# Value projection of the 1024-token set in three column groups (322, 484, 484) instead of four of 322, with the phase's on-chip memory laid out anew

## Chip, cores and metric

One core of a Trainium2 chip runs the whole layer in one launch. The metric is device time in microseconds, the median of three executions. Beside it there is one profiled execution with a trace of every instruction and every DMA.

## What is computed

The layer takes two token sets, x_prompt (1024 tokens) and x_sample (512 tokens), each of width 1024. All weights are shared. Cut to what matters here:

```python
h = rms_norm(x, pre_w)
cols = jnp.einsum('bsd,dc->bsc', h, w_in)          # one combined input projection
m_qk, m_v, m_o, m_z, m_i, m_f, a_qkv, a_z, gate = jnp.split(cols, np.cumsum(IN_SPLITS)[:-1], axis=-1)
y_m = mlstm_mixer(m_qk, m_v, m_o, m_i, m_f, ...) * silu(m_z)      # branch A, uses m_v and the 16 gate columns m_i, m_f
y_a = dilated_attention(a_qkv, rel_table) * silu(a_z)             # branch B, uses the 1536 value columns of a_qkv
merged = sig(g_A) * (y_m @ w_proj_m) + sig(g_B) * (y_a @ w_proj_a)
y = x + rms_norm(merged @ w_out, post_w)
```

The change concerns the first phase of the long set (1024 tokens): the projection of h on 2576 columns of w_in. These are 16 gate columns (m_i, m_f), 1024 columns of m_v and 1536 value columns of the attention.

## The kernel before

**Precision.** Every fp32 operand is split in a high part (a ScalarE copy to fp32r) and a low part (a VectorE subtraction, operand minus high part). `mm3` (L209 to L214) multiplies with three matmuls: high by high, high by low, low by high.

**Seven products.** The long set is two blocks of 512 tokens (rows) by two halves of the contraction (4 tiles of 128 each). The weights of a group are two halves of the contraction by two halves of columns. `value_group` (L452) forms the 2x2 block product with seven block products instead of eight (Winograd's form of Strassen's scheme). In the order of the later groups they are m1, m2, m6, m7, m5, m4, m3. Their left operands H[..][B11 .. B22] are sums of blocks of h, kept for the whole phase; their right operands are sums of weight blocks, made for each group. One product is 4 row tiles t by 4 contraction tiles k by 3 matmuls, so 48 matmuls. The moving operand is the weight block, VW = 322 columns wide, the stationary operand a 128x128 tile of H. A group of two column halves covers 2 x 322 columns; four groups, g = 0 to 3, cover 2576. Each row tile of a product accumulates in one PSUM bank; there are eight in a pool.

**What stands around a product.** `split` (L461) makes the high and low part of a weight block into one of two places (`vhi`, `vlo`, bufs=2), so a block can be split only after the product before the last one, in its place, has ended. `sums` (L442) and L609/L623 form the weight sums on VectorE. The evictions are VectorE additions of PSUM to SBUF tiles `u2`, `u3`, `co` (L626 to L671). `out` (L499) stores a finished piece of 128 rows by 322 columns: m_v columns as high and low parts (through tiles `vz`, `vzm`) to the DRAM tensor `vs`, attention columns to `av`. `opening` (L471) loads the raw weights of the next group with four DMAs on GpSimd's queue and splits its first block; it is called when m4 of a group is issued (L662). The `u2` tiles alternate between the names `u2` and `u2b` from group to group.

**Group 0** is special. Its products are interleaved with the making of H itself: transposes of x on TensorE (`put`, L415), evictions of these by ScalarE and VectorE (L430, L432), differences of the blocks of x (L409, L411). The x tiles of the first block (`x0`) lie in a pool of the left side, those of the second (`x1`) in one of the right side. The `u3` tiles of group 0 are the first 322 columns of the x0 tiles (L2270). The pool `co`, which reuses x1's memory, is opened after m6 (L614).

**Lanes and tables.** `lanes` (L946) makes the decay tables of the mLSTM from the gate columns. It is a generator of five stages with small TensorE transposes (L957, L990, L991, L1011, L1033, L1034) between chains on ScalarE and VectorE. L2284 to L2290 take its steps in groups 1 and 2, after every third product. `bias_tables` (L342) makes the relative-bias rows of the attention with two small matmuls (L356); it runs after the lanes, ahead of group 3.

**Order.** TensorE's instructions stand in the order in which the program issues them. The order on the other engines is planned when the program is built, from dependences and priorities; `issue_after` holds an instruction behind another one on its engine, and `split` has high priority. Memory of a closed pool is reused tile by tile: a new tile waits until the tiles that lay there are done with.

**After the values** come the pairs (L2296 on): `pair_weights` loads and splits two column units (`pw_raw`, `phla`, `phlb`, `psum_w`) in memory that the value weights held, and `unit_pair` multiplies with 512-wide moving operands. The last stores of group 3 go into the list `late` and are issued behind the first pair loads.

Of the kernel before, what the change touches and what calls it, by code (L numbers as in the profile page):

```python
# [29 lines left out]
P = 128  # L30
D = 1024
# [16 lines left out]
VW = 322  # L48
# [25 lines left out]
class Tokens:  # L74


    def __init__(self, dram, S, x, y, name):
        self.S, self.x, self.y, self.n, self.nblk, self.name = S, x, y, S // P, S // BLK, name
        t = lambda shape, what, dt=F32: dram.tile(shape, dt, name=f"{what}_{name}")
        self.qk = t([16, P, S], "qk")  # L80
        self.vs = t([2, S, D], "vs")
        self.G = t([8, P, S], "G")
        self.aqk = t([2, 24, P, S], "aqk")
        self.av = t([S, 1536], "av")
        self.az = t([4, P, S], "az")
# [3 lines left out]
        self.og = t([S, 3, 4, OW], "og")  # L89

# [93 lines left out]
class Net:  # L184
# [157 lines left out]
    def bias_tables(self, sb, ps, dram):  # L342
# [17 lines left out]
        nc.sync.dma_start(self.erow, e)  # L360

# [87 lines left out]
    def value_weights(self, sb):  # L449
        return [sb.tile([P, 2, 4 * VW], F32, name=x, bufs=1) for x in ("va", "vb", "vsum")]  # L450

    def value_group(self, g, T, H, sb, us, co, ps, late=None, begin=None, u3=None, more=None, turn=None):  # L452
# [6 lines left out]
        N = 4 * VW  # L459
        place = lambda: [sb.tile([P, N], F32R, name=x, bufs=2) for x in ("vhi", "vlo")]  # L460
        def split(x, at=None, parts=1):  # L461
            hi, lo = at or place()
            with self.tc.high_priority():
                for i in range(parts):
                    c = slice(i * N // parts, (i + 1) * N // parts)
                    ends = (nc.scalar.activation(hi[:, c], x[:, c], AF.Copy),
                            (nc.gpsimd if i else nc.vector).tensor_sub(lo[:, c], x[:, c], hi[:, c].bitcast(F32)))
            self.splits = ends
            return hi.rearrange("p (k c) -> p k c", c=VW), lo.rearrange("p (k c) -> p k c", c=VW)

        def opening(g):  # L471
            wa, wb = (sb.tile([P, 2, N], F32, name=x, bufs=1) for x in ("va", "vb"))
            for j, w in enumerate((wa, wb)):
                for kh in range(2):
                    nc.gpsimd.dma_start(w[:, kh], self.a["w_vp"][g, j, kh])
            return wa, wb, split(wa[:, 0]), self.splits[1]

        if g:
            wa, wb, w11, early = self.opened
            s = sb.tile([P, 2, N], F32, name="vsum", bufs=1)  # L480
        else:
            first, wa, wb, s, (lead, norm, sub, put) = begin

        def product(m, w, turns=(), outer=False, onto=None):

            banks = onto or [ps.tile([P, BLK], F32, name="d") for _ in range(4)]
            turns = iter(turns)
            if outer:
                next(turns)
            for i in range(4):  # L490
                for j in range(4):
                    t, k = (j, i) if outer else (i, j)
                    ts = slice(t * P, (t + 1) * P)
                    self.mm3(banks[t][:, :VW], (H[0][m][:, k, ts], H[1][m][:, k, ts]), (w[0][:, k], w[1][:, k]),
                             k == 0 and onto is None, k == 3, skip_group_check=onto is not None)
                next(turns, None)
            return banks

        def out(t, blk, jc, c):  # L499

            r = slice(blk * BLK + t * P, blk * BLK + (t + 1) * P)
            c0 = 2 * VW * g + VW * jc
            lo, hi = c0, c0 + VW
            if lo < 16:
                nc.scalar.activation(self.gates_of(T, blk * 4 + t), c[:, 0:16].rearrange("p (j h) -> p j h", h=4), AF.Copy)
            a0, a1 = max(lo, 16), min(hi, 16 + D)
            if a0 < a1:
                w = a1 - a0
                z = vz()
                x = c[:, a0 - c0:a1 - c0]  # L510
                nc.scalar.activation(z[:, 0, :w], x, AF.Copy)
                nc.vector.tensor_sub(z[:, 1, :w], x, z[:, 0, :w].bitcast(F32))
                store(T.vs[:, r, a0 - 16:a1 - 16].rearrange("a t c -> t a c"), z[:, :, :w].bitcast(F32))
            a0 = max(lo, 16 + D)
            if a0 < hi:
                store(T.av[r, a0 - 16 - D:hi - 16 - D], c[:, a0 - c0:])

        vz = lambda: (more.tile([P, 2, VW], F32R, name="vzm", bufs=2) if more and next(turn) < 2 else
                      co.tile([P, 2, VW], F32R, name="vz", bufs=3))
        tile_ = lambda name, bufs: (us if name[:2] == "u2" else co).tile([P, VW], F32, name=name, bufs=bufs)  # L520
        u2 = [tile_(("u2", "u2b")[g % 2], 4) for _ in range(4)]
        add = nc.vector.tensor_add
        if g == 0:
            lead()
            w11, low = split(wa[:, 0], first, 2), []
# [88 lines left out]
            co = co()  # L614
        else:
            with self.tc.issue_after(early.ins):
                self.sums(wa, wb, s)()
            m1 = product(B11, w11)
            for t in range(4):
                nc.scalar.activation(u2[t], m1[t][:, :VW], AF.Copy)  # L620
            w12 = split(wa[:, 1])
            s2 = split(s[:, 1])
            nc.vector.tensor_sub(s[:, 1], wa[:, 1], s[:, 1])  # L623
            yield
            m2 = product(B21, w12)
            co = co()  # L626
            for t in range(4):
                c = tile_("co", 3)
                add(c, u2[t], m2[t][:, :VW])
                out(t, 0, 0, c)  # L630
            yield
            m6 = product(T2, s2)
            for t in range(4):
                add(u2[t], u2[t], m6[t][:, :VW])
            yield
            m7 = product(T3, split(wb[:, 0]))
            u3 = []
            for t in range(4):
                u3.append(tile_("u3", 4))
                nc.vector.tensor_sub(u3[t], u2[t], m7[t][:, :VW])  # L640
            yield
        if g == 0:
            with self.tc.issue_after(low[2]):
                s1 = split(s[:, 0])
        else:
            s1 = split(s[:, 0])
        m5 = product(T1, s1)
        if g == 0:
            for t, c in enumerate(held):
                out(t, 0, 0, c)  # L650
        for t in range(4):
            add(u2[t], u2[t], m5[t][:, :VW])
            c = tile_("co", 3)
# [3 lines left out]
        if late is not None:  # L657
            store = lambda *x: late.append(x)
        m4 = product(T4, split(wb[:, 1]))
        if g < 3:  # L660
            w3 = split(s[:, 1])
            self.opened = opening(g + 1)  # L662
# [5 lines left out]
        m3 = product(B22, w3 if g < 3 else split(s[:, 1]))  # L668
# [277 lines left out]
    def lanes(self, T, sb, bank, apart=False):  # L946
# [8 lines left out]
        li, lf, e, u1, l, q1 = (t(x) for x in ("li", "lf", "e", "u1", "l", "u"))  # L955
# [1249 lines left out]
def body(tc, a):  # L2205
# [3 lines left out]
    with ExitStack() as st:  # L2209
# [12 lines left out]
        with ExitStack() as s1:  # L2222
# [4 lines left out]
            with ExitStack() as sv:  # L2227
                vw = N.pool(sv, "vw", 1, "left")
                us = N.pool(s2, "us", 1, "right")
                s3, s4 = ExitStack(), ExitStack()  # L2230
                begin = [vw.tile([P, 4 * VW], F32R, name=x, bufs=2) for x in ("vhi", "vlo")], *N.value_weights(vw)
# [3 lines left out]
                xp = N.pool(s3, "x0", 1, "left"), N.pool(s4, "x1", 1, "right")  # L2235
                xt = [[xp[i].tile([P, D], F32, name=f"x{i}{t}") for t in range(4)] for i in range(2)]
# [4 lines left out]
                weights = lambda j, kh: nc.sync.dma_start(begin[1 + j][:, kh], a["w_vp"][0, j, kh])  # L2241
# [28 lines left out]
                values = [N.value_group(0, A, H, vw, us, co, ps, None, (*begin, turns), [x[:, :VW] for x in xt[0]])]  # L2270
                next(values[0])
# [3 lines left out]
                for _ in values[0]:  # L2275
                    pass
                s3.close()
                more, turn = N.pool(sv, "more", 1, "left"), itertools.cycle(range(5))
                values += [N.value_group(g, A, H, vw, us, co, ps, late if g == 3 else None, more=more, turn=turn)
                           for g in range(1, 4)]  # L2280
# [221 lines left out]
```

## Time and profile before

| | |
|---|---|
| runs | 2199.57 us median of 3 (2198.99 to 2202.0) |
| profiled execution, its own time | 2196.68 us |
| its span, first to last instruction | 2194.8 us |
| granted TensorE clock, mean | 0.999 |
| PE busy, share of the span | 99% |
| DVE / ACT / POOL busy | 67% / 50% / 32% |
| DMA | 390.42 MB, mean 178 GB/s |

The profiled execution took 2.89 us less than the median of the runs, and 1.9 us more than its span. Busy TensorE is counted with the pipelined ends of matmuls, so the distance between the starts of two matmuls, not their busy time, is what a matmul costs. In the trace, the first phase of the long set runs from the start to the first matmul of the pairs at 235.25 us; of this, m5 of group 0 begins at 60.47 us.

### The profile page before, as it was taken

The page shows a single profiled execution, that of the slowest core. Times are in us where ns is not written, and L with a number is a line of the kernel's source. Part 1 is how long each engine was busy: PE and PEld are TensorE (multiplying, and loading weights), DVE is VectorE, ACT ScalarE, POOL GpSimd, SP SyncE. Part 2 cuts the span into 40 slices and gives each one's busy share as a digit, 9 for nine tenths or more (in the row PEclk, how much of TensorE's full clock was granted, in tenths as well). Part 3 has the DMA queues.
Part 4 walks back from the last instruction along what each step waited for, and adds up shares of the span by engine and source line. Part 5 has one row for each costly group of instructions (what it writes and reads, how often), then busy time and mean ns, then how long its engine had stood idle before and what let it go on. Part 6 is the DMA issues. An engine that isn't in the chain of part 4 may idle for free.

```text
span 2194.8 us, 34409 instructions
## 1 busy us (share of the span) xinstructions
PE 2180.1 (99%) x11962; PEld 1883.1 (86%) x11962; DVE 1460.9 (67%) x2970; ACT 1088.8 (50%) x2246; POOL 706.5 (32%) x994
## 2 busy tenths in 40 slices
PE   9999999999999999999999999999999999999998
PEld 8999888888888888888888889999788888888887
DVE  7775565657787555547888765574667855666673
ACT  7332243344444333446777656666755544554332
POOL 1000432333333222326776650011045522232331
PEclk9999999999999999999999999999999999999999
DMA  3842443433333222366646569997678786776772
GB/s 126 196 116 80 154 165 135 173 106 112 109 115 109 75 86 96 135 217 239 211 155 228 147 191 248 246 244 198 197 238 279 240 282 209 232 258 183 237 244 106
DMA packets 207640, 390.42 MB, mean 178 GB/s; under 512 B 37513, under 2 KB 121161, under 8 KB 207466
## 3 DMA queue, kind: packets, MB, share of 16 engines
q1 hardware_dynamic: 176584, 276.15, 40.5%
q0 software_dynamic: 27280, 99.48, 14.2%
q10 hardware_dynamic: 3602, 12.59, 1.4%
q8 instruction: 95, 1.56, 0.3%
q14 instruction: 79, 0.65, 0.1%
HBM read 274.70 MB, written 113.44 MB: 177 GB/s over the span
## 4 chain that ended last, share of the span: by engine, by line
PE 90%; DMA 4%; DVE 2%; issue 1%; ACT 1%; POOL 1%; SPq 0%; DVEq 0%; POOLq 0%; ACTq 0%
PE d L214 14%; PE d L212 14%; PE d L213 14%; PE dense L212 11%; PE dense L214 11%; PE dense L213 11%; PE lg L1695 1%; PE pt L1725 1%; PE num L212 1%; PE num L214 1%; PE num L213 1%; PE o L1768 1%; PE num L1390 1%; PE a L1097 1%; PE kv L212 1%
## 5 line engine op out<-in xcount | busy, mean ns | idle before, releaser
L212 PE MATMUL dense<-H,wh 128*128 128x512 f32 x664 | 269.4, 406 | 0.0
L213 PE MATMUL dense<-H,wh 128*128 128x512 f32 x664 | 260.4, 392 | 0.0
L214 PE MATMUL dense<-H,wl 128*128 128x512 f32 x664 | 260.3, 392 | 0.0
L213 PE MATMUL d<-Hl,phla 128*128 128x512 f32 x608 | 236.5, 389 | 0.0
L214 PE MATMUL d<-Hh,phla 128*128 128x512 f32 x608 | 236.5, 389 | 0.0
L212 PE MATMUL d<-Hh,phla 128*128 128x512 f32 x608 | 236.5, 389 | 0.0
L281 DVE TENSOR_TENSOR wl<-wraw,wh 128x1024 fp32r<-128x1024 f32 (+1 forms) x121 | 150.1, 1241 | 49.3 <-ACT wh L275 49.0
L214 PE MATMUL d<-Hh,phlb 128*128 128x512 f32 x456 | 177.4, 389 | 0.0
L212 PE MATMUL d<-Hh,phlb 128*128 128x512 f32 x456 | 177.4, 389 | 0.0
L213 PE MATMUL d<-Hl,phlb 128*128 128x512 f32 x456 | 177.4, 389 | 0.0
L275 ACT ACTIVATE wh<-wraw 128x1024 fp32r<-128x1024 f32 (+1 forms) x124 | 128.2, 1035 | 65.6 <-PE dense L213 21.9
L214 PEld LDWEIGHTS dense<-H,wl 128*128 128x128 f32 x664 | 124.7, 188 | 28.1
L697 POOL TENSOR_TENSOR psum_w<-pw_raw 128x512 f32<-128x512 f32 x38 | 55.3, 1455 | 283.3 <-DMA pw_raw<-w_in 266.0
L214 PE MATMUL d<-vhi,Hl 128*128 128x322 f32 x448 | 140.5, 314 | 0.5 <-DVE Hl L432 0.3
L212 PE MATMUL d<-vhi,Hh 128*128 128x322 f32 x448 | 140.3, 313 | 0.1
L213 PE MATMUL d<-vlo,Hh 128*128 128x322 f32 x448 | 139.6, 312 | 0.0
L212 PEld LDWEIGHTS dense<-H,wh 128*128 128x128 f32 x664 | 125.1, 188 | 16.5 <-issue 1.2
L213 PEld LDWEIGHTS dense<-H,wh 128*128 128x128 f32 x664 | 125.3, 189 | 14.7
L1714 DVE CUSTOM_DVE_ANT_0 ls<-lg,bias 128x256 f32<-128x256 f32 (+2 forms) x240 | 78.8, 352 | 85.5 <-PE lg L1695 63.7
L212 PEld LDWEIGHTS d<-Hh,phla 128*128 128x128 f32 x608 | 114.1, 188 | 23.7
L213 PEld LDWEIGHTS d<-Hl,phla 128*128 128x128 f32 x608 | 114.1, 188 | 23.7
L214 PEld LDWEIGHTS d<-Hh,phla 128*128 128x128 f32 x608 | 114.1, 188 | 23.6
(635 smaller groups left out, 5811.1 us busy)
## 6 DMA issues: line engine op xcount, KB each, us to landing
pw_raw<-w_in SPq DMA_DIRECT2D x76, 512.0 KB, 4.3
wraw<-w_in SPq DMA_DIRECT2D x63, 512.0 KB, 4.3
aqk_a<-pwk SPq DMA_DIRECT2D x40, 512.0 KB, 3.5
wraw<-w_pm POOLq DMA_DIRECT2D x24, 512.0 KB, 5.5
wraw<-w_out POOLq DMA_DIRECT2D x24, 512.0 KB, 4.0
aqk_b<-sw SPq DMA_DIRECT2D x40, 256.0 KB, 6.2
wraw<-w_v POOLq DMA_DIRECT2D x22, 430.0 KB, 7.2
qk_a<-pwk SPq DMA_DIRECT2D x16, 512.0 KB, 2.6
```

The source lines that it names most:

```text
L212: nc.tensor.matmul(out, lh, rh, start=start, stop=False, **kw)
L213: nc.tensor.matmul(out, lh, rl, start=False, stop=False, **kw)
L214: nc.tensor.matmul(out, ll, rh, start=False, stop=stop, **kw)
L275: high = nc.scalar.activation(hi[:, :n], raw[:, :n], AF.Copy)
L281: low = (self.lows or nc.vector).tensor_sub(lo[:, :n], raw[:, :n], hi[:, :n].bitcast(F32))
L697: self.nc.gpsimd.tensor_add(s[:, 0], ws[1][:, 0], ws[1][:, 1])
L1097: nc.tensor.matmul(p[:, c - c0], kT[:, ct, c * P:(c + 1) * P], qT[:, ct, c * P:(c + 1) * P], start=ct == 0, stop=ct == 1)
L1390: nc.tensor.matmul(pn, hi[:, j], z[:, c1], start=j == 0 and z is v[0], stop=False)
L1695: nc.tensor.matmul(lg[:, hh], q[hh][:, qs], z.rearrange("p (n j) -> p n j", j=P)[:, pair], start=z is k[hh], stop=z is not k[hh])
L1714: nc.vector.tensor_tensor_reduce(out=ls[rows, hh], in0=ts["lg"][hh][rows, of], in1=bt[rows, hh, by], scale=1.0, scalar=NEG, op0=OP.add, op ...
L1725: nc.tensor.transpose(pp[:, hh * nk + x], ts["ls"][:, hh, x * P:(x + 1) * P], self.ident)
L1768: nc.tensor.matmul(of(hh, 0, P), vh(kt[x], hh), pt[:, hh * len(kt) + x], start=x == 0, stop=x == len(kt) - 1)
```

## The change

The 2576 columns, padded to 2580, are cut in three groups: group 0 stays at 2 x 322 columns and its own code (`value_group`), and groups 1 and 2 take 2 x 484 columns each (`wide_group`). Each group still has seven products of 48 matmuls. `value_split` and `value_product` are the former inner functions `split` and `product`, made methods.

The memory is laid out anew. Four tiles v0 to v3 (8 x 484, 4 x 322, 16 x 484 and 4 x 1024 columns) take the place of `vhi`, `vlo`, `va`, `vb`, `vsum` and x0. In group 0 the places of the split weights lie in v0 and v1, the raw weights and sums in v2, the x0 tiles in v3. In the wide groups the two places of split weights lie in v3 and v0, the four raw blocks in v2, and the sum `ws`, the tiles `wu2` (4), `wco` (2), `wu3` (4) in a new pool on the right side, opened when group 0's pools close. The `wu2` tiles are the same four in both wide groups. The high parts of m_v pieces in group 1 go to three slices of v1 (`z_of`); the low parts are written in place of the piece. The u3 tiles of group 0 move from x0's columns to the pool `co`, which is now opened before the evictions of m7.

The lanes' steps all move into group 2, one after each product, with their tiles in v1 and a tile of the right pool; the bias tables move into group 2 too, their loads after m6, their matmuls after m5, with their tiles in the first raw block. The host lays out the weights for the new groups (`w_vp` for group 0, `w_vw` for the wide ones).

```diff
-VW = 322
+VW, WW = 322, 484
...
+    def wide_open(self, g, wide):
+        if g == 1:
+            quarter = lambda x, i: x[:, i * 4 * WW:(i + 1) * 4 * WW]
+            places = [[quarter(x, i).bitcast(F32R) for i in range(2)] for x in (wide(3), wide(0, False))]
+            self.wide = itertools.cycle(places), [quarter(wide(2, False), i) for i in range(4)]
+        places, raw = self.wide
+        for i in (0, 1, 2, 3) if g == 1 else (0, 2, 3, 1):
+            self.nc.gpsimd.dma_start(raw[i], self.a["w_vw"][g - 1, i // 2, i % 2])
+        with self.tc.issue_after(self.splits[0].ins), self.tc.issue_after(self.splits[1].ins):
+            self.opened = self.value_split(raw[0], next(places)), self.splits[1]
...
+    def wide_group(self, g, T, H, wide, sb, ps, late=None):
...
+        def out(t, blk, jc, c):
+            r = slice(blk * BLK + t * P, blk * BLK + (t + 1) * P)
+            lo = 2 * VW + 2 * WW * (g - 1) + WW * jc - 16
+            hi = min(lo + WW, D + 1536)
+            if lo < D:
+                w = D - lo
+                x, z = c[:, :w], next(z_of)[:, :w]
+                nc.scalar.activation(z, x, AF.Copy)
+                sub(x.bitcast(F32R), x, z.bitcast(F32))
+                for i, y in enumerate((z.bitcast(F32), x)):
+                    store(T.vs[i, r, lo:D], y)
+            a = max(lo, D)
+            store(T.av[r, a - D:hi - D], c[:, a - lo:hi - lo])
+        s0 = sb.tile([P, 4 * WW], F32, name="ws", bufs=1)
+        with self.tc.issue_after(early.ins):
+            add(s0, b0, b1)
+            sub(b0, a0, b0)
+            sub(a0, s0, a0)
+        m1 = product(B11, w11)
+        u2 = tiles("wu2")
+        for t in range(4):
+            nc.scalar.activation(u2[t], m1[t][:, :WW], AF.Copy)
+        w12 = split(a1)
+        s2 = split(a0)
+        sub(a1, a1, a0)
+        yield
+        m2 = product(B21, w12)
+        for t in range(4):
+            c = sb.tile([P, WW], F32, name="wco", bufs=2)
+            add(c, u2[t], m2[t][:, :WW])
+            out(t, 0, 0, c)
+        yield
...
-    def value_group(self, g, T, H, sb, us, co, ps, late=None, begin=None, u3=None, more=None, turn=None):
+    def value_group(self, T, H, us, co, ps, begin, wide):
...
+            co = co()
+            u3 = [co.tile([P, VW], F32, name="u3", bufs=4) for _ in range(4)]
             for t in range(4):
                 nc.vector.tensor_sub(u3[t], u2[t], m7[t][:, :VW])
...
-                next(values[1])
-                with ExitStack() as s4:
-                    lanes = N.lanes(A, N.pool(s4, "lane", 1, "right"), lambda: ps.tile([P, BLK], F32, name="d"))
-                    for g in range(1, 3):
-                        for j, _ in enumerate(values[g]):
-                            if j % 3 == 0:
-                                with tc.issue_after(N.splits[0].ins), tc.issue_after(N.splits[1].ins):
-                                    next(lanes, None)
...
+                for _ in N.wide_group(1, A, H, wide, sb, ps):
+                    pass
+                last = N.wide_group(2, A, H, wide, sb, ps, late)
+                lanes = N.lanes(A, Carve(part(1), sb.tile([P, P], F32, name="l_more")), lambda: ps.tile([P, BLK], F32, name="d"))
+                tables = N.bias_tables(Carve(N.wide[1][0]), ps, dram)
+                for j in range(7):
+                    next(last)
+                    with tc.issue_after(N.splits[0].ins), tc.issue_after(N.splits[1].ins):
+                        next(lanes, None)
+                    if j in (2, 4):
+                        next(tables)
...
```

The rest of `wide_group` follows the later groups of the former `value_group`, in the same order of products.

More of the change, by code (lines that the diff above doesn't have):

```diff
@@ L89, in __init__, with tile @@
         self.og = t([S, 3, 4, OW], "og")
+class Carve:
+    def __init__(self, *parts):
+        self.free = [[x, 0, x.shape[-1]] for x in parts]
+    def tile(self, shape, dt, name=None, bufs=1):
+        n = math.prod(shape[1:])
+        part = next(p for p in self.free if p[1] + n <= p[2])
+        x = part[0][:shape[0], part[1]:part[1] + n].bitcast(dt)
+        part[1] += -(-n // 8) * 8
+        names = "abcdefgh"[:len(shape) - 1]
+        return x if len(shape) == 2 else x.rearrange(f"p ({' '.join(names)}) -> p {' '.join(names)}", **dict(zip(names, shape[1:])))
 class Rot:
@@ L447, in sums, with value_split @@
         return lambda: nc.vector.tensor_sub(s[:, 1], s[:, 0], wa[:, 0])
-    def value_weights(self, sb):
-        return [sb.tile([P, 2, 4 * VW], F32, name=x, bufs=1) for x in ("va", "vb", "vsum")]
-    def value_group(self, g, T, H, sb, us, co, ps, late=None, begin=None, u3=None, more=None, turn=None):
+    def value_split(self, x, at, parts=1):
+        nc, (hi, lo) = self.nc, at
+        N = hi.shape[-1]
+        with self.tc.high_priority():
+            for i in range(parts):
+                c = slice(i * N // parts, (i + 1) * N // parts)
+                ends = (nc.scalar.activation(hi[:, c], x[:, c], AF.Copy),
+                        (nc.gpsimd if i else nc.vector).tensor_sub(lo[:, c], x[:, c], hi[:, c].bitcast(F32)))
+        self.splits = ends
+        return [z.rearrange("p (k c) -> p k c", k=4) for z in at]
@@ new lines, in value_product @@
+    def value_product(self, H, m, w, ps, turns=(), outer=False, onto=None):
+        W = w[0].shape[-1]
+        banks = onto or [ps.tile([P, BLK], F32, name="d") for _ in range(4)]
+        turns = iter(turns)
+        if outer:
+            next(turns)
+        for i in range(4):
+            for j in range(4):
+                t, k = (j, i) if outer else (i, j)
+                ts = slice(t * P, (t + 1) * P)
+                self.mm3(banks[t][:, :W], (H[0][m][:, k, ts], H[1][m][:, k, ts]), (w[0][:, k], w[1][:, k]),
+                         k == 0 and onto is None, k == 3, skip_group_check=onto is not None)
+            next(turns, None)
+        return banks
@@ new lines, in wide_group @@
+    def wide_group(self, g, T, H, wide, sb, ps, late=None):
+        nc = self.nc
+        add, sub = nc.vector.tensor_add, nc.vector.tensor_sub
+        places, (a0, a1, b0, b1) = self.wide
+        if g == 1:
+            z = wide(1)
+            z_of = itertools.cycle([z[:, i * 400:(i + 1) * 400].bitcast(F32R) for i in range(3)])
+        store = nc.sync.dma_start
+        split = lambda x: self.value_split(x, next(places))
+        product = lambda m, w: self.value_product(H, m, w, ps)
+        tiles = lambda name: [sb.tile([P, WW], F32, name=name, bufs=4) for _ in range(4)]
+        w11, early = self.opened
+        def out(t, blk, jc, c):
[23 more added lines that the diff above has]
+        sub(a1, a1, a0)
+        yield
+        m2 = product(B21, w12)
[3 more added lines that the diff above has]
+            out(t, 0, 0, c)
+        yield
+        m6 = product(T2, s2)
+        for t in range(4):
+            add(u2[t], u2[t], m6[t][:, :WW])
+        yield
+        m7 = product(T3, split(b0))
+        u3 = tiles("wu3")
+        for t in range(4):
+            sub(u3[t], u2[t], m7[t][:, :WW])
+        yield
+        m5 = product(T1, split(s0))
+        for t in range(4):
+            add(u2[t], u2[t], m5[t][:, :WW])
+            c = sb.tile([P, WW], F32, name="wco", bufs=2)
+            add(c, u3[t], m5[t][:, :WW])
+            out(t, 1, 1, c)
+        yield
+        if late is not None:
+            store = lambda *x: late.append(x)
+        m4 = product(T4, split(b1))
+        w3 = split(a1)
+        if g == 1:
+            self.wide_open(2, wide)
+        for t in range(4):
+            add(u3[t], u3[t], m4[t][:, :WW])
+            with self.tc.issue_after(self.splits[0].ins):
+                out(t, 0, 1, u3[t])
+        yield
+        m3 = product(B22, w3)
+        yield
+        for t in range(4):
+            add(u2[t], u2[t], m3[t][:, :WW])
+            out(t, 1, 0, u2[t])
@@ L457, in value_group @@
+    def value_group(self, T, H, us, co, ps, begin, wide):
         nc = self.nc
         store = nc.sync.dma_start
[L459 to L497, printed above, removed]
+        places, wa, wb, s, (lead, norm, sub, put) = begin
@@ L507, in out @@
[L507 to L521, printed above, removed]
+            a0 = max(lo, 16)
+            w = hi - a0
+            z = co.tile([P, 2, VW], F32R, name="vz", bufs=3)
+            x = c[:, a0 - lo:]
+            nc.scalar.activation(z[:, 0, :w], x, AF.Copy)
@@ L613, in value_group @@
             yield
[L614 to L645, printed above, removed]
+        with self.tc.issue_after(low[2]):
             s1 = split(s[:, 0])
         m5 = product(T1, s1)
-        if g == 0:
-            for t, c in enumerate(held):
-                out(t, 0, 0, c)
+        for t, c in enumerate(held):
+            out(t, 0, 0, c)
         for t in range(4):
             add(u2[t], u2[t], m5[t][:, :VW])
-            c = tile_("co", 3)
+            c = co.tile([P, VW], F32, name="co", bufs=3)
             add(c, u3[t], m5[t][:, :VW])
@@ L656, in value_group @@
         yield
[L657 to L658 removed]
         m4 = product(T4, split(wb[:, 1]))
[L660 to L662 removed]
+        w3 = split(s[:, 1])
+        self.wide_open(1, wide)
         for t in range(4):
@@ L667, in value_group @@
         yield
-        m3 = product(B22, w3 if g < 3 else split(s[:, 1]))
+        m3 = product(B22, w3)
         yield
```

61 lines of the change are left out of this document (33 added, 28 removed).

## The prediction

> **What bounds the kernel now.** I read the page first, its busy shares and the chain of work that ended last, then the timeline of TensorE around the value groups.
>
> ```profile
> span 2194.8 us, 34409 instructions
> ...
> PE 2180.1 (99%) x11962; PEld 1883.1 (86%) x11962; DVE 1460.9 (67%) x2970; ACT 1088.8 (50%) x2246; POOL 706.5 (32%) x994
> ...
> PE 90%; DMA 4%; DVE 2%; issue 1%; ACT 1%; POOL 1%; SPq 0%; DVEq 0%; POOLq 0%; ACTq 0%
> ...
> L214 PE MATMUL d<-vhi,Hl 128*128 128x322 f32 x448 | 140.5, 314 | 0.5 <-DVE Hl L432 0.3 <-DVE Hl L390 0.2
> ```
>
> TensorE is busy for 99% of the span and carries 90% of the chain. The value matmuls of the long set are 3 x 448 = 1344 (four groups of 336), and the engine sat idle ahead of their third part for only 0.5 us in all. So this phase costs what its matmuls cost, and a change pays if it takes time out of that row of matmuls without opening a gap in it. The mean of 314 ns is pipelined busy time and says nothing of the pace; that comes from starts in the timeline.
>
> ```profile
> 60.47 0.31 PE L212 MATMUL d<-vhi,Hh 128*128 128x322 f32 x1
> ...
> 96.36 0.27 PE L957 MATMUL d<-ident,gall 128*128 128x128 f32 x1
> 96.39 0.39 PE L212 MATMUL d<-vhi,Hh 128*128 128x322 f32 x1
> ...
> 139.69 0.21 PE L990 MATMUL d<-ident,l_u 64*1 64x64 f32 x1
> ...
> 599.73 0.39 PE L212 MATMUL d<-Hh,phla 128*128 128x512 f32 x1
> ...
> 605.17 0.39 PE L212 MATMUL d<-Hh,phlb 128*128 128x512 f32 x1
> ...
> 1323.56 0.36 PE L214 MATMUL dense<-wh,H 128*128 128x430 f32 x1
> ...
> 1324.74 0.35 PE L214 MATMUL dense<-wh,H 128*128 128x430 f32 x1
> ```
>
> The first two stretches hold five and six whole products of 48 matmuls, 528 in 35.89 + 43.30 us: 0.1500 us for one of 322 columns, with no gap. The third holds 24 matmuls of 512 columns in 5.44 us: 0.2267 each. The fourth holds six of 430 columns in 1.18 us: 0.1967 each. Columns go up by 1.59 from 322 to 512, time only by 1.51: some of a matmul's cost does not depend on its width. That part is what fewer, wider matmuls save.
>
> **The change, part by part.** *Fewer matmuls.* Groups 1 to 3 are 1008 matmuls of 322 columns, 1008 x 0.1500 = 151.2 us. In their place come two groups, 672 matmuls of 484 columns. No row has 484. Between its neighbours 430 and 512 a straight line gives 0.1967 + 54 x 0.000366 = 0.2165, so 145.5 us and 5.7 us less. The line from 322 to 512 gives 0.2154, 144.7 us, 6.5 less; the line from 322 through 430, carried on, gives 0.2200, 147.9 us, 3.3 less. I take the neighbours: 5.7. A product then lasts 48 x 0.2165 = 10.4 us instead of 7.2.
>
> The Trainium skill (TensorE: Matmul & The Clock Gate, section "Wait — 56ns, not 53.3ns?") puts a warm matmul at N divided by 2.4 GHz plus about 2.5 ns, whatever its width. By it 322 columns would take 136.7 ns and 484 would take 204.2, the groups 137.8 and 137.2 us, and the change would be worth 0.6 us. The trace does not agree: 150.0 ns at 322 and 226.7 at 512, each some 13 ns over the rule.
>
> *Work beside the products.* The wider blocks make every split, sum and eviction longer.
>
> ```profile
> L467 DVE TENSOR_TENSOR vlo<-vsum,vhi 128x1288 fp32r<-128x1288 f32 x12 | 18.0, 1496 | 13.9 <-ACT vhi L466 13.9
> L466 ACT ACTIVATE vhi<-vsum 128x1288 fp32r<-128x1288 f32 x12 | 15.4, 1280 | 29.6 <-PE d L214 29.6
> L728 DVE TENSOR_TENSOR c<-pu,d 128x512 f32<-128x512 f32 x15 | 10.4, 690 | 26.0 <-PE d L214 25.8
> L664 DVE TENSOR_TENSOR u<-u,d 128x322 f32<-128x322 f32 x12 | 5.9, 489 | 8.4 <-PE d L214 8.4
> ...
> 62.00:140.00 78.00, 59.24 (x114) 1.00 0.68 167
> ```
>
> The last line is a window's VectorE busy time: 59.24 of 78 us, 76%, with the lanes in it. A block of 1936 columns instead of 1288 scales the low part to 2.25 us and the high part to 1.92. An eviction of 484 columns lies between 489 and 690 ns, about 0.66. A wide group has on VectorE 7 low parts and 4 sums, 11 x 2.25 = 24.8, and 28 evictions, 18.5: 43.3 of its 72.7 us. That is cover enough. A split takes 4.2 us from the moment its place comes free, which is one whole product (10.4 us) ahead of its use; before it was 2.8 of 7.2. I cost it at nothing; without that cover each of the 14 splits would cost TensorE up to 4.2 us.
>
> *Loads and stores.* The queues involved:
>
> ```profile
> vs_a<-vz SPq DMA_DIRECT2D x13, 322.0 KB, 7.1
> vb<-w_vp POOLq DMA_DIRECT2D x6, 644.0 KB, 6.4
> av_a<-co SPq DMA_DIRECT2D x16, 161.0 KB, 1.9
> vs_a<-vzm SPq DMA_DIRECT2D x3, 322.0 KB, 8.6
> ```
>
> A raw block is now 968 KB, by size 9.6 us. The last of the four waits for the split of m3's weights, which happens at the start of m4. That leaves m4, m3 and the next m1 and m2 before its sum is used in m6: over 35 us after group 0. GpSimd has nothing else queued behind these loads in the value phase. They cost nothing.
>
> The pieces of group 1 that hold m_v have two `wco` tiles, three before (`co`). So the third and fourth addition after m2 wait for the stores of the first and second, and the low part for m7 stands behind them on VectorE. A row tile ends every 2.6 us. The second piece leaves about 2.3 us after its tile's end (addition, copy, subtraction, issue), so the fourth addition can run at 7.5 us plus the landing time after m2's start; with it and the split's 2.25 us the weights of m7 are ready 10.4 us plus the landing time after m2's start. They are due at 20.8. At the 7.1 us of the row 3.3 us are left. The single set of `wu2` tiles makes ScalarE's copies of the next m1 wait for the stores of m3's pieces, a full product (10.4 us) earlier, against about 2.3 + 7.1: also covered, and the next high part is placed ahead of these copies.
>
> *Group 0.* The u3 subtractions (L606) must now wait until all of x1's columns are read, which the last transposes of T2 do.
>
> ```profile
> 48.21 0.60 PE L423 MATMUL d<-ident,x 128*128 128x128 f32 x4
> 48.56 0.39 PE L212 MATMUL d<-vhi,Hh 128*128 128x322 f32 x1
> ...
> 50.54 0.31 PE L213 MATMUL d<-vlo,Hh 128*128 128x322 f32 x1
> 51.14 0.41 PE L214 MATMUL d<-vhi,Hl 128*128 128x322 f32 x1 [0.29 <-DVE Hl L432]
> 51.39 0.39 PE L427 MATMUL d<-Hh,Hl 128*128 128x512 f32 x1
> ...
> 44.41 0.88 DVE L606 TENSOR_TENSOR x<-u,d 128x322 f32<-128x322 f32 x2
> ...
> 50.00 0.48 DVE L606 TENSOR_TENSOR x<-u,d 128x322 f32<-128x322 f32 x1
> 50.40 0.69 DVE L432 TENSOR_TENSOR Hl<-d,Hh 128x512 fp32r<-128x512 f32 x1
> ```
>
> Here VectorE is the bound: m6's first 12 matmuls take from 48.56 to 51.39, 2.83 instead of 1.8 us, and wait for T2's last low part, which stands behind a u3 subtraction. Moved behind it, the four subtractions leave room, and up to 1.0 us goes. If they stay ahead of it, all four come after 48.8 and add up to 4 x 0.48 = 1.9. I take 0.4 off, since they have no earlier use than m6's evictions; m7's banks come free later, and T2's own banks then carry m6.
>
> *Lanes and tables.* TensorE's instructions there are the same ones, moved. Between the lanes' steps stand one product, in the chain's long step two, instead of three or six.
>
> ```profile
> 100.31 0.31 ACT L963 ACTIVATE l_e<-l_e 64x128 f32<-64x128 f32 x1
> ...
> 106.65 0.21 DVE L965 TENSOR_SCALAR l_u<-l_e 64x128 f32<-64x128 f32 x1
> ...
> 121.15 0.14 DVE L986 TENSOR_TENSOR l_tt<-l_u,l_l 64x1 f32<-64x1 f32 x1
> ```
>
> The long step runs from the transpose at 96.36 to 121.3, 24.9 us. Now the transposes that use it stand after m6, two products (20.8 us) behind. But before nothing used it until 139.69, and VectorE took it up only 6.0 us after ScalarE's part. Taken up at once it ends after 18.9 us. The tables' loads (one of `oh`, eight small ones of `tb`) pass on SyncE between the stores of m6 and m5, with two products until their matmul. I put 0.4 us for waits here and at `wco` together.
>
> *The pairs* reuse v2 and v3. Their first raw load waits for m3's weights to be split, about 4.2 us into m4, 16 us ahead of the first pair; `psum_w` waits for m4's end, 10.4 us ahead.
>
> ```profile
> 229.11 2.18 POOL L697 TENSOR_TENSOR psum_w<-pw_raw 128x512 f32<-128x512 f32 x1 [62.77 <-DMA pw_raw<-w_in]
> 231.37 1.29 POOL L698 TENSOR_TENSOR psum_w<-psum_w,pw_raw 128x512 f32<-128x512 f32 x1
> ...
> 232.69 1.06 ACT L678 ACTIVATE phla<-psum_w 128x1024 fp32r<-128x1024 f32 x1 [3.80 <-POOL psum_w L698]
> ...
> 233.78 1.23 DVE L679 TENSOR_TENSOR phla<-psum_w,phla 128x1024 fp32r<-128x1024 f32 x1 [3.64 <-ACT phla L678]
> ```
>
> From 229.11 to 235.01 this takes 5.9 us; 10.4 are there. Nothing.
>
> *Sum.* -5.7 - 0.4 + 0.4 = -5.7. The profiled execution of 2196.68 would become 2191.0; it lies 2.89 below the median of the runs, so on their scale 2199.57 - 5.7 = 2193.9.
>
> **The rivals.** *The lanes' chain, stretched, stops TensorE* (slower). VectorE's instructions among which the chain queues are 484/322 = 1.5 times longer. If the chain stretches with them, 24.9 becomes 37.4 us, and TensorE stands at the transposes after m6 for 16.6 us: -5.7 + 16.6 = +10.9, 2210.5. For it: the chain's order is planned, each step waits for its own last result, and it queues behind the last split by `issue_after`. Against: VectorE has 43.3 + at most 14.7 (106.65 to 121.3, other work included) of 72.7 us, 80%, hardly more than the 76% of before. It eats the whole gain from a chain of 26.5 us. *The chain as slow as before*, 24.9: TensorE waits 4.1, total -1.6, 2198.0. *The change saves nothing on TensorE*, because a matmul costs by its columns alone: 484 columns at 0.1500 x 484/322 = 0.2255 make 151.5 us, +0.3, 2199.9. The 512 row speaks against it (0.2385 by that rule, 0.2267 measured). This is also close to what the skill's rule leaves. *The two `wco` tiles* stop VectorE: at a landing time of 12 us instead of 7.1, TensorE waits 1.6 at m7 and the total is -4.1, 2195.5; a wait of this kind takes the whole gain from a landing of 16 us.
>
> **How the numbers follow.** A measurement of this kernel can tell 0.2%, 4.4 us, from no change; -5.7 passes this by only 1.3. Forecast 0.60, of which 0.53 ends faster and 0.07, with a pace towards 0.2200, within the bound; slow chain 0.09, cost by columns 0.06, `wco` 0.06, all within it; stretched chain 0.19, slower. So faster 0.53, same 0.28, slower 0.19. Low end: -6.5 - 1.0, less 1.5 (half the runs' spread of 3.0), 2190.6. High end, leaving out the stretched chain: +0.3 + 1.9 in group 0, plus 1.5: 2203.3.
>
> **What would show it.** Right: rows of 672 matmuls of 484 columns at starts 0.2165 us apart, the first pair about 6 us before 235.25, no idle time of TensorE at L990, L1011 or L1033. Wrong: a pace at or above 0.2200; a gap of TensorE ahead of the lanes' transposes with VectorE as releaser; a wait of m7 in group 1 with VectorE waiting for stores of `wco`; m6 of group 0 beginning later than at 48.56 or its first 12 matmuls longer than 2.83 us.

## The result and the profile after

The changed kernel takes 2209.41 us (median; 2204.85 to 2212.51), the kernel before 2199.28 on the same chip: a ratio of 1.0043 [1.0029, 1.0056], slower by 10.1 us where 5.7 less was forecast. A repetition gave 2208.68 against 2199.88, 1.0039 [1.0025, 1.0054]. The profiled execution of the changed kernel took 2210.11 us.

The page has the same face as before. TensorE is busy for 99% of a longer span:

```profile
span 2208.3 us, 33612 instructions
...
PE 2182.9 (99%) x11626; PEld 1862.4 (84%) x11626; DVE 1457.6 (66%) x2923; ACT 1086.6 (49%) x2227; POOL 702.9 (32%) x990
...
PE 89%; DMA 6%; DVE 2%; issue 1%; ACT 1%; POOL 1%; SPq 0%; DVEq 0%; POOLq 0%; ACTq 0%
...
L228 PE MATMUL d<-v,Hh 128*128 128x484 f32 (+1 forms) x336 | 121.5, 361 | 4.6 <-DVE v L474 4.6
L227 PE MATMUL d<-v,Hh 128*128 128x484 f32 (+1 forms) x336 | 122.3, 364 | 2.9 <-ACT v L473 2.7
```

The share of DMA in the chain went from 4% to 6%, and the value matmuls now have idle time ahead of them, 4.6 and 2.9 us, where one third of them had 0.5 before. TensorE's timeline shows where (start, duration, line, operation, and in brackets the idle time and what ended it):

```profile
81.89 0.38 PE L227 MATMUL d<-v,Hh 128*128 128x484 f32 x1
...
92.43 0.38 PE L227 MATMUL d<-v,Hh 128*128 128x484 f32 x1
94.44 0.48 PE L228 MATMUL d<-v,Hh 128*128 128x484 f32 x1 [1.63 <-DVE v L474]
...
104.64 0.38 PE L229 MATMUL d<-v,Hl 128*128 128x484 f32 x1
107.72 0.48 PE L227 MATMUL d<-v,Hh 128*128 128x484 f32 x1 [2.70 <-ACT v L473]
111.18 0.77 PE L228 MATMUL d<-v,Hh 128*128 128x484 f32 x1 [2.98 <-DVE v L474]
111.75 0.61 PE L229 MATMUL d<-v,Hl 128*128 128x484 f32 x1
...
117.00 0.38 PE L227 MATMUL d<-v,Hh 128*128 128x484 f32 x1
...
242.47 0.40 PE L227 MATMUL d<-Hh,phla 128*128 128x512 f32 x1
```

The wide groups begin at 81.89, as before's group 1 did (81.98). Then m2 waits for the low part of its weights, and m6 for both parts of its own. Start to start, less the 0.22 us that a matmul takes, the four gaps of over 0.3 us from 92.43 on are 1.79, 2.87, 3.24 and 0.35 us, 8.25 together. From 111.75 to 117.00 there are 13 starts, 0.404 us apart, at nearly half pace: 13 x 0.184 is another 2.4 us. The pairs begin at 242.47 instead of 235.25, 7.2 us later. The rest of the phase runs with no wait, the transposes of the lanes included.

The weights of m2 are a raw block, not a sum. Their high part stood on ScalarE behind a copy of a finished piece of group 0, which waited for a store out of a `vz` tile to land (the low part followed on VectorE at 92.21):

```profile
89.90 0.46 ACT L608 ACTIVATE vz<-u 128x306 fp32r<-128x306 f32 x1 [1.70 <-DMA vs_a<-vz]
...
90.37 1.81 ACT L473 ACTIVATE v<-v 128x1936 fp32r<-128x1936 f32 x1
```

The weights of m6 are late because the sums that make them are. VectorE's timeline:

```profile
94.30 0.86 DVE L609 TENSOR_TENSOR vz<-u,vz 128x306 fp32r<-128x306 f32 x2
99.23 2.18 DVE L537 TENSOR_TENSOR ws<-v 128x1936 f32<-128x1936 f32 x1 [4.07 <-DMA vs_a<-vz]
101.44 2.17 DVE L538 TENSOR_TENSOR v<-v 128x1936 f32<-128x1936 f32 x1
103.65 2.17 DVE L539 TENSOR_TENSOR v<-ws,v 128x1936 f32<-128x1936 f32 x1
...
108.96 2.17 DVE L474 TENSOR_TENSOR v<-v,v 128x1936 fp32r<-128x1936 f32 x1
```

The three sums of group 1 start at 99.23, after the last low parts of group 0 (L609 at 94.30) and after 4.07 us of waiting for a store out of `vz`: `ws` lies on the memory of the `vz` tiles. In the kernel before the same sums stood among the last pieces of group 0 and began 21 us earlier; the pieces themselves ended at nearly the same time as now:

```profile
77.78 1.49 DVE L445 TENSOR_TENSOR vsum<-vb 128x1288 f32<-128x1288 f32 x1
...
81.20 1.49 DVE L446 TENSOR_TENSOR vb<-va,vb 128x1288 f32<-128x1288 f32 x1
82.61 1.49 DVE L447 TENSOR_TENSOR vsum<-vsum,va 128x1288 f32<-128x1288 f32 x1
...
93.83 0.48 DVE L512 TENSOR_TENSOR vz<-u,vz 128x306 fp32r<-128x306 f32 x1 [0.64 <-ACT vz L511]
```

The chain of waits of the changed kernel says why the last pieces come late:

```profile
69.17 12.92 DMA vs_a<-vz
82.19 0.48 ACT vz L608
82.70 0.51 DVE vz L609
83.22 4.43 DMA vs_a<-vz
87.73 0.47 ACT vz L608
88.22 0.49 DVE vz L609
88.73 4.61 DMA vs_a<-vz
...
95.25 3.85 DMA vs_a<-vz
99.23 2.19 DVE ws L537
```

There are three `vz` tiles. Each takes a piece's copy (ScalarE) and low part (VectorE), and goes to memory before the next piece can have it. One such store took 12.92 us. The windows from 70 to 82 us show what it met (PE, PEld, DVE, ACT, POOL busy, then granted clock, DMA share, GB/s), the changed kernel first:

```profile
70.00:82.00 12.00, 12.00 (x83) 12.00 (x82) 4.93 (x7) 1.79 (x3) 0.54 (x1) 1.00 1.01 262
```

```profile
70.00:82.00 12.00, 12.00 (x83) 12.00 (x82) 8.61 (x14) 3.43 (x7) 0.00 (x0) 1.00 0.51 123
```

A raw block of group 1 is 968 KB instead of 644, and the last of the four was issued at 70.95 us instead of 63.55. So loads were still under way until 81 us, where the last had landed at 72 before. Three stores were issued between 65.8 and 69.2 us; they landed in 11.0, 12.1 and 12.9 us, and those of the kernel before, issued from 65.6 to 69.1, in 7.8, 9.5 and 6.7. VectorE did 4.93 us of work in these 12, where it had done 8.61: it was short of something to do, not of time. But the kernel before has the same three tiles, and its last piece was done less than 1 us earlier. So what is new is mainly that the sums stand behind the pieces, not that the pieces are late.

### The profile page after: what moved, and what is told of

Same layout as the page of the kernel before. It is cut to its first block, busy times and chain, and to the rows that moved or that the text cites. A ratio compares the mean times of both kernels' runs of the same rounds, so it can differ in the third digit from the quotient of the medians.

```text
span 2208.3 us, 33612 instructions
## 1 busy us (share of the span) xinstructions
PE 2182.9 (99%) x11626; PEld 1862.4 (84%) x11626; DVE 1457.6 (66%) x2923; ACT 1086.6 (49%) x2227; POOL 702.9 (32%) x990
## 4 chain that ended last, share of the span: by engine, by line
PE 89%; DMA 6%; DVE 2%; issue 1%; ACT 1%; POOL 1%; SPq 0%; DVEq 0%; POOLq 0%; ACTq 0%
PE d L229 13%; PE d L228 13%; PE d L227 13%; PE dense L227 11%; PE dense L228 11%; PE dense L229 11%; PE lg L1754 1%; DMA sraw<-ym_a 1%; DMA vs_a<-vz 1%; PE pt L1784 1%; DMA V0b<-aqk_a 1%; PE num L227 1%; PE num L229 1%; PE num L228 1%; DMA og_a<-ot 1%
## 5 line engine op out<-in xcount | busy, mean ns | idle before, releaser
L774 POOL TENSOR_TENSOR psum_w<-pw_raw,psum_w 128x512 f32<-128x512 f32 x38 | 49.3, 1297 | 253.1 <-DVE phla L738 253.1
L228 PE MATMUL d<-v,Hh 128*128 128x484 f32 (+1 forms) x336 | 121.5, 361 | 4.6 <-DVE v L474 4.6
L227 PE MATMUL d<-v,Hh 128*128 128x484 f32 (+1 forms) x336 | 122.3, 364 | 2.9 <-ACT v L473 2.7
```

The source lines that it names most:

```text
L227: nc.tensor.matmul(out, lh, rh, start=start, stop=False, **kw)
L228: nc.tensor.matmul(out, lh, rl, start=False, stop=False, **kw)
L774: nc.gpsimd.tensor_sub(s[:, 1], wa[:, 1], s[:, 1])
```

## Experiments

My theory was that group 1's sums wait for group 0's last pieces (A). The rival was that VectorE has too much to do in the wide groups (B). Each edit is against the changed kernel, unless said.

**Low parts in place, six tiles for the high parts.** A piece's low part overwrites the piece, and its high part has a tile of its own, so six pieces can be under way instead of three. All sums, splits and evictions stay as wide as they are. A piece also leaves in two stores of half the size.

```diff
-            z = co.tile([P, 2, VW], F32R, name="vz", bufs=3)
+            z = co.tile([P, VW], F32R, name="vz", bufs=6)[:, :w]
...
-            nc.vector.tensor_sub(z[:, 1, :w], x, z[:, 0, :w].bitcast(F32))
+            nc.vector.tensor_sub(x.bitcast(F32R), x, z.bitcast(F32))
```

> Edit: in group 0 the low part of an m_v piece is written in place of the piece, and the high part goes to one of six 322-column tiles instead of three of 2 x 322, in the same memory. Theory A (stores: the four 968 KB loads and the stores fill the DMA rings, three vz tiles hold up ScalarE and VectorE, so the last vz store of group 0 goes out at 95 us, lands at 99, and the weight sums of group 1, whose tile lies over vz, start 7 us late): the last store goes out before 90 us, the first sum of group 1 starts before 95, TensorE's waits at m2 and m6 of group 1 (1.8, 2.9 and 3.2 us) fall below 2 us together, the pairs begin at 232 to 235 us instead of 242.5, and the run is 7 us or more faster than the changed kernel. Theory B (VectorE has too much to do in group 1: three sums and three low parts of 2.2 us before m6 can run): the waits stay at 6 us or more and the pairs begin at 240 or later.

2197.75 against 2199.86 us, 0.9993 [0.9983, 1.0002]. No wait of TensorE of over 0.3 us is left in the wide groups. VectorE's timeline:

```profile
88.36 0.47 DVE L609 TENSOR_TENSOR u<-u,vz 128x306 fp32r<-128x306 f32 x1
89.49 2.18 DVE L537 TENSOR_TENSOR ws<-v 128x1936 f32<-128x1936 f32 x1 [0.66 <-DMA vs_a<-u]
```

The last low part begins at 88.36, where the last two began at 94.30 in the changed kernel, and the sums start at 89.49, still behind it, but in time. B falls: the wide work is all there and costs TensorE nothing.

**Less to load.** Of two raw blocks of group 1 only the last quarter is loaded.

> Edit: of the last two raw blocks of group 1 only a quarter is loaded, 1.45 MB less; the rest of these blocks holds old values, so group 1's results are left wrong. Theory A: the vz stores of group 0 land in 8 us or less instead of 12.9, the first sum of group 1 starts before 95 us, the waits of TensorE in group 1 fall from 8.2 us to below 3, pairs before 237 us. Theory B: the loads have landed before the sums anyway, so the waits stay at 6 us or more.

2206.82 us, 1.0033 [1.0022, 1.0045]. On the chain of waits the stores out of `vz` now landed in 8.34, 4.46, 5.42 and 2.80 us, the longest 4.6 us sooner. The wait in m2 was gone, but `ws` moved only from 99.23 to 96.83, and 5.0 of the 8.25 us of waits remained, between what the two theories had expected. The size of the loads is a part of it, not all.

**`ws` elsewhere.** Two layouts that take `ws` off the `vz` tiles. The first allots `wu3`, one `wco` and `wu2` ahead of it:

```diff
+        u3, early_c = None, []
+        if g == 1:
+            u3, early_c = tiles("wu3"), [sb.tile([P, WW], F32, name="wco", bufs=2)]
+        u2 = tiles("wu2")
         s0 = sb.tile([P, 4 * WW], F32, name="ws", bufs=1)
```

> Edit: only the order in which the tiles of the right pool are laid out (wu3, wco, wu2, ws instead of ws, wu2, wco, wu3), so that the sum ws no longer lies over vz but over u2 and u2b. Theory A: the sum starts when the last VectorE subtraction of group 0 is done, about 95 us, not when its store has landed at 99.2; the waits at m6 fall by about 4 us, the pairs begin at 238 to 239.5. Theory B: no difference, 242 us.

The second also allots a `vz` tile ahead of group 0's `u3` and `u2b` ahead of `u2`, leaves `wu2` behind `ws`, and puts the lanes' tile first.

> Edit: only memory places change against the changed kernel: u2b is laid ahead of u2, vz ahead of u3 and co in group 0, and in the right pool l_more, wu3, wco, ws, wu2, so that ws lies over the end of u3, co and u2b and no longer over vz or u2. The three double vz tiles stay, and so does the filling of the DMA rings. If the place of ws alone makes the loss (theory A, narrowed: the stores were as late before, but nothing waited for them), the first sum starts at 82 to 88 us, TensorE waits less than 1 us in group 1, pairs at 232 to 233.5. If the few vz tiles are needed for the loss too (ScalarE and VectorE held up in order), the waits are 2 us or more and the pairs begin after 234.5.

The first gave 2202.52 us, 1.001 [1.0, 1.0019], pairs at 237.46; the second 2201.94, 1.0005 [0.9995, 1.0015], pairs at 237.19. VectorE's timeline of the second:

```profile
92.20 2.18 DVE L474 TENSOR_TENSOR v<-v,v 128x1936 fp32r<-128x1936 f32 x1 [0.94 <-ACT v L473]
94.29 0.86 DVE L612 TENSOR_TENSOR vz<-u,vz 128x306 fp32r<-128x306 f32 x2
95.07 2.17 DVE L540 TENSOR_TENSOR ws<-v 128x1936 f32<-128x1936 f32 x1
```

The 4 us of waiting for the store are gone, and the pairs begin 5.3 us sooner than in the changed kernel. But `ws` starts in the instant in which the last piece is done. In this kernel the sum names no semaphore but those of the two raw loads, and there is no idle time ahead of it: what keeps it until 95.07 is its place in VectorE's order, behind the pieces. So the late start of the sums has two parts: order (to 95) and memory (to 99). The wait in m2 is still there, at 1.0 us: the ring of three tiles is as it was.

**Both cures**: in place with five tiles, a fourth `co` tile, and a layout like the second's.

> Edit: in-place low parts with five high tiles and four co tiles in group 0, and a layout in which ws lies over co and u2b, which are free earliest. Theory A: no wait of TensorE over 0.5 us in group 1, pairs begin at 231 to 233 us (3.4 us ahead of the kernel before: 1008 x 0.1500 against 672 x 0.2200), clock at 1.00 throughout the value phase; total 2194 to 2198 us if the later stretch at 1458 us behaves as before. Theory B: waits of 4 us or more stay, pairs after 238.

2199.55 us, 0.9993 [0.9984, 1.0002]; `ws` at 89.58, pairs at 232.24. No wait is left, and the layout adds nothing once the pieces come early. The total missed the 2194 to 2198 us that were expected: the pairs are 3.0 us earlier than before's, the median only 0.3, though its interval reaches 3.5.

**The wait put into the kernel before.** Only the order is changed there: the sums of group 1 stand behind the last low part of group 0.

```diff
-            with self.tc.issue_after(early.ins):
+            with self.tc.issue_after(early.ins), (self.tc.issue_after(self.last_low.ins) if g == 1 else ExitStack()):
```

> Edit to the kernel before: the weight sums of group 1 (L445 to L447, at 77.8 to 84.1 us) may not start before group 0's last vz subtraction (93.8 us in the trace before), nothing else. Theory A: the kernel before loses about what the changed one does, 4 to 7 us at m6 of group 1 plus a lower clock, pairs at 239 to 243. Theory B (it is the width of the work): three sums of 1.5 us are caught up, less than 2 us.

2204.72 against 2200.77 us, 1.0021 [1.0012, 1.0031]. The timeline of TensorE:

```profile
96.89 0.27 PE L957 MATMUL d<-ident,gall 128*128 128x128 f32 x1
98.42 0.41 PE L212 MATMUL d<-vhi,Hh 128*128 128x322 f32 x1 [1.26 <-ACT vhi L466]
99.95 0.42 PE L213 MATMUL d<-vlo,Hh 128*128 128x322 f32 x1 [1.12 <-DVE vlo L467]
```

Here too m6 of group 1 waits for its high part and then for its low part. Pairs come at 240.14, 4.9 us late, in a kernel with no wide matmul and no new layout. The two waits are 2.9 us of this; the 17 matmuls from 99.95 to 104.10 lose another 1.6, at a granted clock of 0.58 between 100 and 104. The order of the sums alone is enough to lose.

**A plain delay.** The kernel before, with m1 of group 3 multiplied twice.

> Edit to the kernel before: in group 3 the product m1 is issued twice, the first result unread: 48 matmuls, 7.2 us on TensorE and nothing else. Pairs at 242.5, as in the changed kernel. If a shift by itself makes the later attention stages lose more (3 us at 1459 us in the changed kernel), the run is 10 us or more slower; if the later loss is the scatter of a stage in which the DMA rings are full, it is 7.2 us slower within 1.5.

Pairs at 242.18, +6.9 us; 2208.87 against 2200.77 us, 1.0041 [1.0028, 1.0054], +8.1. A delay ahead of the pairs is carried to the end nearly as it is.

**Another cut**: 264, 512 and 512 columns, with low parts in place, a layout like the second's, and no `wco` tiles (these pieces lie in `wu3` and `ws`).

> Edit: the cut 264 / 512 / 512 instead of 322 / 484 / 484 on the layout of ws over free memory, with in-place low parts; c of m2 in wu3, c of m5 in ws, no wco. 336 matmuls of 264 columns at about 0.1225 (the 258-column rows stand 0.120 apart) instead of 0.150, 672 of 512 at 0.2267 instead of 0.2200: -9.2 + 4.5 = -4.7 us against e4_fixed if TensorE stays the bound, pairs at 227 to 228.5; if VectorE binds group 0's first half (its work there does not shrink with the columns, about 4 products of 7.2 us), half of the 9.2 is lost and the pairs begin at 232. Rival on the pace: if 484 columns are slow because of their row pitch and 264 is no better than its columns, 264 comes out at 0.130 or more.

2199.79 us, 0.9994 [0.9983, 1.0006]; pairs at 231.23, the earliest of all, but not at the 228 to 229 that 0.227 us for each matmul give. The 672 matmuls started 0.2306 us apart on average (median 0.229) with no idle time ahead of any; what stretched them was not found. The 264 columns took 0.121 us, near the 0.1225 expected.

**The changed kernel and the first version once more**, on one chip with the kernel before.

> The changed kernel once more, beside the next one and the kernel before on the same chip. Open: whether its end is as late as its pairs (+7.2 us) or later than that (the six runs said +10.1). If only the stretch up to the pairs costs, and the rest is the scatter of the attention stage, the median is 7 to 8.5 us above the kernel before. If the changed layout also costs something behind the pairs, it is 9.5 or more above. The pairs should again begin at 242 to 243, with the same three waits in m2 and m6 of the first wide group.

> The version with six tiles for the high parts and the low parts written in place, once more. Its pairs began 2.7 us earlier than before's. If that carries to the end, the median is 2 to 3 us below the kernel before, a ratio of 0.9987 to 0.9991; if wider matmuls give back nothing at the end, it is within 1 us. Against the changed kernel of the same call it should be 9 to 11 us faster.

The changed kernel: pairs at 241.65, the same three waits (0.96, 3.15, 3.24), +8.8 us, which lies between the two cases that were expected. With low parts in place: pairs at 232.12, 2197.44 against 2199.88 us, 0.9985 [0.9974, 0.9996], faster by 2.4 us. It beats the changed kernel by 11.2 us and the one before by 0.15%; the earlier comparison had 0.07%, with an interval that takes in 1.

Over the runs the start of `ws` orders the waits of TensorE in group 1 (those in m2 included) and, but for 0.3 us among the first three, the start of the pairs. Only gaps of over 0.3 us are counted:

| | `ws` starts | waits | pairs |
|---|---|---|---|
| in place, six tiles, once more | 88.87 | 0 | 232.12 |
| in place, six tiles | 89.49 | 0 | 232.54 |
| both cures | 89.58 | 0 | 232.24 |
| `ws` elsewhere, second | 95.07 | 3.0 | 237.19 |
| `ws` elsewhere, first | 95.31 | 3.2 | 237.46 |
| less to load | 96.83 | 5.0 | 238.99 |
| the change, once more | 98.41 | 7.7 | 241.65 |
| the change | 99.23 | 8.25 | 242.47 |

## Why the prediction was wrong

**The step that failed** is "Loads and stores ... They cost nothing", and with it "I cost it at nothing" for the work beside the products. I counted how much VectorE has to do in a wide group and when a raw block is free, and both were near enough: the 43.3 us left out the eight low parts of m_v pieces of 0.56 each, and VectorE was busy for 47.50 of the 73 us from 82 to 155 with the low parts in place. I did not ask when group 1's first sums and splits can start: what lies in the memory that `ws` takes, what stands ahead of them on VectorE and ScalarE, and how long the stores of group 0 take beside loads of 968 KB. Before, the sums stood at 77.78 and 82.61 in the trace, with the last piece at 93.83 behind them; that order was a cover that I used without naming it. And the split of m2's weights, which I had put at 4.2 us from the moment its place comes free, began on ScalarE only at 90.37, 8.5 us after the last matmuls of group 0 (81.89). The price was 10.65 us, 8.25 of waits and 2.4 at half pace.

**The pace** was mis-sized. The undisturbed version settles it: from its first wide matmul at 82.71 to its pairs at 232.54 it takes 149.8 us, of which 1.7 are the lanes' and tables' small matmuls, so 148.1 / 672 = 0.2204 us for 484 columns. That is just above the largest of my three values (0.2200, the line from 322 through 430 carried on), not the neighbours' 0.2165. A pace at or above 0.2200 was one of my signs of being wrong. In the kernel before, 81.98 to 235.25 is 153.3 us with the same 1.7. The saving is 3.4 us, not 5.7. The Trainium skill (TensorE: Matmul & The Clock Gate, section "Wait — 56ns, not 53.3ns?") would have 0.2042 for 484 columns, an estimate by its rule; the measurement disagrees with it here as at 322 and 512 (there by 13.3 and 10.9 ns, not by 13 each).

**The sum then is** -0.1 at the start of group 1, -3.4 of pace, +10.65: +7.2, which is where the pairs stand. The median is 10.1 later, 8.8 in the repetition. 1.2 more than its shift came in the plain delay as well. In the profile of the change a part of the remainder is in the attention stage, where the DMA share is 1.05 (1440 to 1456 us; also 1.05 from 1432 to 1449 in the kernel before). The waits of TensorE from 1440 to 1466 us:

```profile
PE lg L1754 <- DMA V0a<-aqk_a: 2.8, 1, 2.8
PE lg L1754 <- DMA V0b<-aqk_a: 0.6, 1, 0.6
```

The same two transfers cost TensorE 1.2 and 0.8 us in the repetition, 0.6 and 0.9 in the plain delay, and the second alone 0.4 in the kernel before. With them the granted clock fell to 0.79 (in the kernel before it was 1.00 from 1449 to 1460):

```profile
1456.00:1466.00 10.00, 6.57 (x32) 5.84 (x31) 4.86 (x23) 3.23 (x11) 0.00 (x0) 0.79 0.96 242
```

With 0.96 from 1466 to 1500 that is at most some 3.5 us, an estimate, as TensorE was idle for part of it. With 3.0 us more of waits and the 7.2 at the pairs, it makes up about the 13.5 us between the two profiled spans. Whether the change adds anything there beyond the delay is open: 1 to 2 us is less than what the runs of one kernel differ by.

**Group 0**: the 0.4 us did not come off. m6 begins at 48.64 instead of 48.56, and its first 12 matmuls take 2.83 us as before; the gap in them is 0.52 us now, 0.45 before.

**The lanes and the tables** moved without cost; the 0.4 us put for waits there and at `wco` was not needed. No idle time of TensorE stands at their transposes, so the rival of the stretched chain, which had nearly the right time (2210.5), was right by accident and its mechanism is refuted; the slow chain too. **The two `wco` tiles** did make VectorE wait for stores, 1.2 us after m2 of group 1 and 2.6 us once after an m5, and nothing of it reached TensorE. **Cost by columns** would be 0.2255; 0.2204 was measured. None of my rivals was what happened.

## What to carry to other kernels

When memory is laid out anew, ask of each new tile what lay there last, which store or subtraction ends that, and what stands ahead of the tile's first writer on its engine; a total of busy time answers none of it. Larger loads lengthen the stores that run beside them (the longest took 12.92 us here and 8.34 with less to load), and a small ring of store tiles passes that on to everything that stands behind the pieces. A gain of 2% in the pace of one phase (3.4 of 153 us) is used up by two waits of 2 us: a memory place that lets a sum go ahead can be worth more than wider matmuls.

## What the hardware showed that I had not expected

After the waits of 2.87 and 3.24 us in m6 the matmuls of 484 columns ran 0.404 us apart for 5.3 us, and the granted clock in that window was 0.74:

```profile
104.00:117.00 13.00, 7.32 (x21) 5.55 (x19) 11.47 (x10) 5.01 (x5) 1.08 (x2) 0.74 0.47 152
```

So two waits of 6.1 us together cost 8.5. A shorter wait did it as well: in the second layout a single one of 1.9 us at 107.02 was followed by matmuls 0.404 us apart from 108.24 to 111.47, while the wait of 1.79 in m2 of the changed kernel was not. In the kernel before no wait in groups 1 to 3 passed 0.3 us, so this did not show. Stores of 306 and 322 KB landed in 3.4 to 12.9 us in one and the same phase, the longest while the DMA share was 1.01. And a matmul's time over its columns is not a straight line: 0.121 us at 264, 0.150 at 322, 0.1967 at 430, 0.2204 at 484, 0.2267 at 512 in the pairs but 0.2306 on average in the value phase.
